# ReLU and row sums: the first 128 rows on 32 partitions, handled by VectorE alone

## The chip, the cores and the metric

The kernel runs on one core of a Trainium2 chip. The metric is the device time of one execution in microseconds (us), the median of several runs; less is better. The work is done by VectorE (DVE in the profile), ScalarE (ACT) and the DMA engines; SyncE (SP) only waits and issues transfers.

## The reference

```
x = np.random.randn(32, 512, 1024).astype(np.float32)

def reference(x):
    relu_x = np.maximum(x, 0)
    return np.sum(relu_x, axis=-1).astype(np.float32)
```

The input is 16,384 rows of 1,024 numbers, 67.1 MB. Each row is rectified and summed to one number; the output is 64 KB.

## The kernel before

Seen as 16,384 rows, the input is cut into three regions of 128 x 1, 128 x 111 and 128 x 16 rows (`REGIONS`). In each, partition p of the on-chip memory takes as many consecutive rows as the region has per partition: one, 111 or 16. The sums go to `res`, 128 partitions by 128 columns, and are stored from there.

**Loads.** Three big buffers (`buf[:, 0..2]`), each 16 rows per partition, are filled in turn by seven chunks (`CHUNKS`, line 94): chunk 0 is the first region's one row and 15 rows of the second region, in two DMAs; chunks 1 to 6 have 16 rows each. The remaining 16 rows per partition are the tail: pieces of 8, 4 and 2 rows (line 104), and two last rows cut into pieces of less than a row (lines 115 and 118), so that little is left to compute when the last bytes land. All loads are issued by SP on one queue. Chunks 0, 1 and 2 are issued at once; chunk 0's two DMAs are moved to the front of the program. From chunk 3 on, SP first waits until the reductions of the chunk that was in the same buffer are done (`s_dve`, line 90); the tail waits for chunk 4's.

**Compute.** In chunks 0 to 5, ScalarE rectifies several rows in place with one instruction (line 154, `ACT_STEPS`) and VectorE sums these rows with `tensor_reduce` (line 169, `DVE_STEPS`). In chunk 5 a few rows, and in chunk 6 and the tail all rows, are done one at a time, rectified and summed by one instruction, by either engine (`on_act`, line 130; `on_dve`, line 133).

**Stores.** The first region's sums lie in column 0 of `res`, one on each partition. VectorE transposes 32x32 blocks of `res` after chunk 1 (line 178), which puts the 128 sums into four rows of 32 in `turned`; SP waits for that (`s_turn`) behind the tail loads and stores four pieces of 128 B (line 120). It then waits for chunk 6 and the last load and stores the second region's columns (line 126), and at the very end the third region's (line 224). The program ends when all stores have landed.

Of the kernel before, what the change touches and what calls it, by code (L numbers as in the profile page):

```python
# [3 lines left out]
P = 128  # L4
D = 1024
BIG = 16
NB = 3
REGIONS = [1, 111, 16]
CHUNKS = [[(0, 0, 1), (1, 0, 15)]] + [[(1, 16 * c + 15, 16)] for c in range(6)]
ACT_STEPS = [[16], [7, 9], [7, 9], [7, 9], [4, 5, 7], [3, 4, 5]]  # L10
DVE_STEPS = [[16], [7, 4, 5], [7, 4, 5], [7, 4, 5], [4, 5, 7], [3, 4, 5]]
TAIL = [8, 4, 2]
CUT = 912
HEAD = 224
# [4 lines left out]
def bass_relu_sum_kernel(  # L19
# [14 lines left out]
    fp32 = mybir.dt.float32  # L34
    ALU = mybir.AluOpType
    AF = mybir.ActivationFunctionType
    X = mybir.AxisListType.X

    B, S, _ = x.shape
    J = B * S // P  # L40
    NBIG = len(CHUNKS)
    assert BIG * NBIG + sum(TAIL) + 2 == J == sum(REGIONS)

    xr = x.rearrange("b s d -> (b s) d")
    of = out.rearrange("b s -> (b s)")
    start = [sum(REGIONS[:i]) for i in range(len(REGIONS))]
    xv = [
        xr[P * s : P * (s + n), :].rearrange("(p j) d -> p j d", p=P)
        for s, n in zip(start, REGIONS)
    ]  # L50
    ov = [of[P * s : P * (s + n)].rearrange("(p j) -> p j", p=P) for s, n in zip(start, REGIONS)]

    buf = nc.alloc_sbuf_tensor("buf", [P, NB, BIG, D], fp32)
    w = D - CUT
    seam = nc.alloc_sbuf_tensor("seam", [P, 2 + w + HEAD + 3], fp32)
    res = nc.alloc_sbuf_tensor("res", [P, J], fp32)
    turned = nc.alloc_sbuf_tensor("turned", [P, 32], fp32)
    aside = nc.alloc_psum_tensor("aside", [P, 4 * D], fp32)

    n_in = NBIG + len(TAIL) + 3  # L60
    s_in = [nc.alloc_semaphore(f"s_in{i}") for i in range(n_in)]
    s_act = nc.alloc_semaphore("s_act")
    s_dve = nc.alloc_semaphore("s_dve")
# [2 lines left out]
    s_half = nc.alloc_semaphore("s_half")  # L66
    s_seam = nc.alloc_semaphore("s_seam")
    s_last = nc.alloc_semaphore("s_last")
    s_turn = nc.alloc_semaphore("s_turn")
    s_store = nc.alloc_semaphore("s_store")  # L70
    s_out = nc.alloc_semaphore("s_out")

    sp, act, dve = nc.sync, nc.scalar, nc.vector

    NTWO = len(ACT_STEPS)
    done = [sum(map(len, DVE_STEPS[: c + 1])) for c in range(NTWO)]

# [4 lines left out]
    code = nc.main_func.blocks[0].instructions  # L82
    arrival = next(
        i
        for i, ins in enumerate(code)
        if ins.engine == mybir.EngineType.SP and type(ins).__name__ == "InstDrain"
    )
    for c in range(NBIG + 1):
        if c >= NB:
            sp.wait_ge(s_dve, done[c - NB])  # L90
        if c < NBIG:
            i = 0
            for g, j, n in CHUNKS[c]:
                sp.dma_start(  # L94
                    out=buf[:, c % NB, i : i + n, :], in_=xv[g][:, j : j + n, :]
                ).then_inc(s_in[c], 16)
                i += n
                if c == 0:
                    code.insert(arrival, code.pop())
                    arrival += 1  # L100
    r = 0
    tail = []
    for i, n in enumerate(TAIL):
# [10 lines left out]
    for k, (lo, hi) in enumerate((first, second, third)):  # L114
# [1 line left out]
            s_in[NBIG + len(TAIL) + k], 16  # L116
        )
    sp.dma_start(out=seam[:, 2 : 2 + w + HEAD], in_=rows[:, CUT : D + HEAD]).then_inc(s_seam, 16)
    sp.wait_ge(s_turn, 1)
    sp.dma_start(  # L120
        out=of[0:P].rearrange("(k q) -> k q", q=32), in_=turned[0:P:32, 0:32]
    ).then_inc(s_store, 16)
    sp.wait_ge(s_fact, 1)
    sp.wait_ge(s_fdve, 1)
# [4 lines left out]
    def on_act(t, acc, to=None):  # L129
        return act.activation(t if to is None else to, t, AF.Relu, accum_out=acc)  # L130

    def on_dve(t, acc, to=None):
        return dve.tensor_scalar(  # L133
            out=t if to is None else to,
            in0=t,
            scalar1=0.0,
            scalar2=None,
            op0=ALU.max,
            op1=ALU.add,
            accum_out=acc,  # L140
        )

    def row(c, i):
        return buf[:, c % NB, i, :], res[:, c * BIG + i : c * BIG + i + 1]

    k = 0
    for c in range(NTWO):
        alone = BIG - sum(ACT_STEPS[c])
        act.wait_ge(s_in[c], 16 * len(CHUNKS[c]))
        r = 0  # L150
        ready = []
        for n in ACT_STEPS[c]:
            t = buf[:, c % NB, r : r + n, :]
            act.activation(t, t, AF.Relu).then_inc(s_act, 1)  # L154
            k += 1
            ready += [k] * n
            r += n
        for i in range(BIG - alone // 2, BIG):
            on_act(*row(c, i))
        if alone:  # L160
            dve.wait_ge(s_in[c], 16 * len(CHUNKS[c]))
            for i in range(BIG - alone, BIG - alone // 2):
                on_dve(*row(c, i))
        r = seen = 0
        for n in DVE_STEPS[c]:
            if ready[r + n - 1] > seen:
                seen = ready[r + n - 1]
                dve.wait_ge(s_act, seen)
            dve.tensor_reduce(  # L169
                out=res[:, c * BIG + r : c * BIG + r + n],  # L170
                in_=buf[:, c % NB, r : r + n, :],
                axis=X,
                op=ALU.add,
            ).then_inc(s_dve, 1)
            r += n
        if c == 1:
            dve.wait_ge(s_dve, done[c])
            dve.transpose(out=turned[:, :], in_=res[:, 0:32]).then_inc(s_turn, 1)  # L178


    j0 = NBIG * BIG
    for c in range(NTWO, NBIG):
        act.wait_ge(s_in[c], 16 * len(CHUNKS[c]))
        dve.wait_ge(s_in[c], 16 * len(CHUNKS[c]))
        for i in range(BIG):
            ins = (on_act if i % 2 else on_dve)(*row(c, i))
            if i >= BIG - 2:
                ins.then_inc(s_fact if i % 2 else s_fdve, 1)
# [16 lines left out]
    k = 2 + w  # L205
# [49 lines left out]
```

## Time and profile before

| | |
|---|---|
| median of 3 runs | 160.74 us (160.72 to 160.82) |
| the profiled execution | 160.78 us, of which the span shows 159.4 |
| VectorE busy | 120.7 us (76%) |
| ScalarE busy | 101.4 us (64%) |
| DMA queue of SP | 67.18 MB in 2,456 packets, 98.0% of the time of 16 DMA engines |
| first load (512 KB), issue to landing | 3.4 us |
| last load | lands at 156.84 us by the chain; VectorE's last addition starts at 157.53 |

The span runs from the first recorded instruction to the end of the last event; the run's time has 1.4 us more around it. A packet in the DMA records is one contiguous run of bytes that one of the 16 DMA engines moves: a load of n rows to each of 128 partitions has 128 packets of n x 4 KB. "SPq" is SP's issuing of a DMA; the time to landing counts from there and holds the wait in the queue behind earlier transfers.

### The profile page before, as it was taken

How to read it: one execution, taken by the hardware profiler on the slowest of the kernel's cores; microseconds unless marked ns; L12 is line 12 of the kernel's file. 1: busy time of each engine (PE TensorE's matmuls, PEld its weight loads, DVE VectorE, ACT ScalarE, POOL GpSimd, SP SyncE). 2: the span in 40 equal slices, each digit the busy share in tenths (PEclk: the TensorE clock that was granted, in tenths of full speed). 3: DMA queues.
4: the chain of work that ended last, by engine and by line, in shares of the span. 5: the costliest groups of instructions: out<-in, count | busy, mean ns of one | idle time of the engine just before them, and what ended most of it. 6: DMA issues, size and time to landing. Idle time of an engine off the chain costs nothing.

```text
span 159.4 us, 150 instructions
## 1 busy us (share of the span) xinstructions
DVE 120.7 (76%) x59; ACT 101.4 (64%) x54; POOL 0.2 (0%) x4
## 2 busy tenths in 40 slices
DVE  0000000009999999999999999999999999898995
ACT  3000059990799808996099951999329990496975
POOL 0000000000000000000000000000000000000000
DMA  9997996996997998989969969969969979798994
GB/s 378 493 401 339 493 526 263 526 526 263 526 460 329 526 411 378 526 362 428 526 296 493 526 263 526 526 263 526 510 280 526 444 345 526 304 485 366 423 399 146
DMA packets 2457, 67.18 MB, mean 421 GB/s; under 512 B 536, under 2 KB 792, under 8 KB 1176
## 3 DMA queue, kind: packets, MB, share of 16 engines
q1 hardware_dynamic: 2456, 67.18, 98.0%
q14 instruction: 1, 0.01, 0.0%
HBM read 67.11 MB, written 0.07 MB: 421 GB/s over the span
## 4 chain that ended last, share of the span: by engine, by line
DVE 54%; DMA 34%; ACT 9%; SPq 1%; issue 0%
DVE res L169 54%; DMA buf<-in_x_dram 34%; ACT buf L154 9%; SPq L104 1%; SPq L115 0%; DVE seam L133 0%; SPq L94 0%; ACT aside L130 0%; DVE turned L178 0%
## 5 line engine op out<-in xcount | busy, mean ns | idle before, releaser
L169 DVE TENSOR_REDUCE res<-buf 128x4 f32<-128x4096 f32 (+4 forms) x16 | 99.3, 6276 | 35.6 <-ACT buf L154 35.6
L154 ACT ACTIVATE buf<-buf 128x7168 f32<-128x7168 f32 (+5 forms) x13 | 80.4, 6233 | 46.2 <-DMA buf<-in_x_dram 46.2
L133 DVE TENSOR_SCALAR_CACHE_REDUCE buf<-buf 128x1024 f32<-128x1024 f32 (+3 forms) x20 | 20.9, 1100 | 1.6 <-DMA buf<-in_x_dram 1.4
L130 ACT ACTIVATE buf<-buf 128x1024 f32<-128x1024 f32 x14 | 14.6, 1042 | 7.9 <-DMA buf<-in_x_dram 7.9
L130 ACT ACTIVATE aside<-buf 128x1024 f32<-128x1024 f32 (+2 forms) x5 | 4.1, 828 | 1.1 <-DMA buf<-in_x_dram 1.0
L130 ACT ACTIVATION_READ_ACCUMULATOR buf<-buf 128x1 f32 x14 | 2.6, 186 | 0.0
L154 ACT ACT_TABLE_LOAD x1 | 1.3, 1283 | 1.3 <-PEq L240 1.3
L133 DVE DVE_READ_ACCUMULATOR buf<-buf 128x1 f32 x20 | 1.7, 83 | 0.0
L130 ACT ACTIVATION_READ_ACCUMULATOR aside<-buf 128x1 f32 x5 | 0.9, 187 | 0.0
L133 DVE TENSOR_SCALAR_CACHE_REDUCE seam<-seam 128x227 f32<-128x227 f32 x1 | 0.4, 391 | 0.0
L130 ACT ACTIVATE aside<-seam 128x114 f32<-128x114 f32 x1 | 0.3, 270 | 0.0
L178 DVE STREAM_TRANSPOSE turned<-res 128x32 f32<-128x32 f32 x1 | 0.2, 213 | 0.0
L130 ACT ACTIVATION_READ_ACCUMULATOR aside<-seam 128x1 f32 x1 | 0.2, 186 | 0.0
L240 POOL MEMSET const-bfloat16-1.0<- 128x1 bf16 x1 | 0.1, 102 | 0.0
L240 POOL MEMSET const-uint8-127<- 128x1 uint8 x1 | 0.1, 102 | 0.0
L240 POOL MEMSET const-float32-1.0<- 128x1 f32 x1 | 0.1, 99 | 0.0
L240 POOL MEMSET const-float32-0.0<- 128x1 f32 x1 | 0.1, 98 | 0.2 <-issue 0.2
L133 DVE DVE_READ_ACCUMULATOR seam<-seam 128x1 f32 x1 | 0.1, 82 | 0.0
## 6 DMA issues: line engine op xcount, KB each, us to landing
buf<-in_x_dram SPq DMA_DIRECT2D x1, 7680.0 KB, 21.2
buf<-in_x_dram SPq DMA_DIRECT2D x1, 4096.0 KB, 25.5
buf<-in_x_dram SPq DMA_DIRECT2D x1, 2048.0 KB, 30.0
buf<-in_x_dram SPq DMA_DIRECT2D x1, 1024.0 KB, 32.0
buf<-in_x_dram SPq DMA_DIRECT2D x1, 512.0 KB, 3.4
buf<-in_x_dram SPq DMA_DIRECT2D x1, 456.0 KB, 32.6
buf<-in_x_dram SPq DMA_DIRECT2D x1, 312.0 KB, 33.0
seam<-in_x_dram SPq DMA_DIRECT2D x1, 168.0 KB, 32.6
```

The source lines that it names most:

```text
L104: sp.dma_start(out=buf[:, tb, r : r + n, :], in_=xv[-1][:, r : r + n, :]).then_inc(s_in[NBIG + i], 16)
L130: return act.activation(t if to is None else to, t, AF.Relu, accum_out=acc)
L133: return dve.tensor_scalar(out=t if to is None else to, in0=t, scalar1=0.0, scalar2=None, op0=ALU.max, op1=ALU.add, accum_out=acc,)
L154: act.activation(t, t, AF.Relu).then_inc(s_act, 1)
L169: dve.tensor_reduce(out=res[:, c * BIG + r : c * BIG + r + n], in_=buf[:, c % NB, r : r + n, :], axis=X, op=ALU.add,).then_inc(s_dve, 1)
L178: dve.transpose(out=turned[:, :], in_=res[:, 0:32]).then_inc(s_turn, 1)
L240: nc = _bacc.Bacc("TRN2", target_bir_lowering=False, num_devices=1)
```

## The change

The first 128 rows are no longer a part of chunk 0, one row to each of 128 partitions. They are loaded first of all into partitions 0 to 31, four consecutive rows (16 KB) to each, in the first part of buffer 2, which chunk 2 fills later. VectorE alone handles them, with two instructions: a `tensor_scalar` that rectifies all four rows of the 32 partitions in place, and a `tensor_reduce` that sums them into `lead`, 32 partitions by four numbers. Neither ScalarE nor a transpose is needed for them, and SP stores `lead` in 32 pieces of 16 B at the place where it stored `turned`. Chunk 0 keeps its 15 rows of the second region in one DMA, so ScalarE and VectorE handle 15 rows there instead of 16. SP now waits, before it issues chunk 2's load, until VectorE has done the two instructions (`s_led`). The loads at the front of the program are this lead load and chunk 0's.

```diff
-CHUNKS = [[(0, 0, 1), (1, 0, 15)]] + [[(1, 16 * c + 15, 16)] for c in range(6)]
-ACT_STEPS = [[16], [7, 9], ...
-DVE_STEPS = [[16], [7, 4, 5], ...
+LEAD = 4
+CHUNKS = [(1, 0, 15)] + [(1, 16 * c + 15, 16) for c in range(6)]
+ACT_STEPS = [[15], [7, 9], ...
+DVE_STEPS = [[15], [7, 4, 5], ...
...
+    leaders = P // LEAD
+    fore = buf[:leaders, NB - 1, :LEAD, :]
+    sp.dma_start(
+        out=fore, in_=xr[:P, :].rearrange("(p j) d -> p j d", j=LEAD)
+    ).then_inc(s_lead, 16)
+    ahead()
     for c in range(NBIG + 1):
+        if c == NB - 1:
+            sp.wait_ge(s_led, 2)
         if c >= NB:
             sp.wait_ge(s_dve, done[c - NB])
         if c < NBIG:
-            i = 0
-            for g, j, n in CHUNKS[c]:
-                sp.dma_start(
-                    out=buf[:, c % NB, i : i + n, :], in_=xv[g][:, j : j + n, :]
-                ).then_inc(s_in[c], 16)
-                i += n
-                if c == 0:
-                    code.insert(arrival, code.pop())
-                    arrival += 1
+            g, j, n = CHUNKS[c]
+            sp.dma_start(
+                out=buf[:, c % NB, BIG - n :, :], in_=xv[g][:, j : j + n, :]
+            ).then_inc(s_in[c], 16)
+            if c == 0:
+                ahead()
...
-    sp.wait_ge(s_turn, 1)
     sp.dma_start(
-        out=of[0:P].rearrange("(k q) -> k q", q=32), in_=turned[0:P:32, 0:32]
+        out=of[:P].rearrange("(p j) -> p j", j=LEAD), in_=lead[:leaders, :]
     ).then_inc(s_store, 16)
...
+    dve.wait_ge(s_lead, 16)
+    dve.tensor_scalar(out=fore, in0=fore, scalar1=0.0, scalar2=None, op0=ALU.max).then_inc(s_led, 1)
+    dve.wait_ge(s_led, 1)
+    dve.tensor_reduce(out=lead[:leaders, :], in_=fore, axis=X, op=ALU.add).then_inc(s_led, 1)
+
     k = 0
     for c in range(NTWO):
...
-        if c == 1:
-            dve.wait_ge(s_dve, done[c])
-            dve.transpose(out=turned[:, :], in_=res[:, 0:32]).then_inc(s_turn, 1)
```

`ahead()` does what the two removed lines did: it moves the DMA just written to the front of the program. The new local names `bare` and `ready = [0] * bare` only shift chunk 0's rows by one place in its buffer.

More of the change, by code (lines that the diff above doesn't have):

```diff
@@ L8 @@
 REGIONS = [1, 111, 16]
-CHUNKS = [[(0, 0, 1), (1, 0, 15)]] + [[(1, 16 * c + 15, 16)] for c in range(6)]
-ACT_STEPS = [[16], [7, 9], [7, 9], [7, 9], [4, 5, 7], [3, 4, 5]]
-DVE_STEPS = [[16], [7, 4, 5], [7, 4, 5], [7, 4, 5], [4, 5, 7], [3, 4, 5]]
+LEAD = 4
+CHUNKS = [(1, 0, 15)] + [(1, 16 * c + 15, 16) for c in range(6)]
+ACT_STEPS = [[15], [7, 9], [7, 9], [7, 9], [4, 5, 7], [3, 4, 5]]
+DVE_STEPS = [[15], [7, 4, 5], [7, 4, 5], [7, 4, 5], [4, 5, 7], [3, 4, 5]]
 TAIL = [8, 4, 2]
@@ L56, in bass_relu_sum_kernel @@
     res = nc.alloc_sbuf_tensor("res", [P, J], fp32)
-    turned = nc.alloc_sbuf_tensor("turned", [P, 32], fp32)
+    lead = nc.alloc_sbuf_tensor("lead", [P, LEAD], fp32)
     aside = nc.alloc_psum_tensor("aside", [P, 4 * D], fp32)
@@ L68, in bass_relu_sum_kernel @@
     s_last = nc.alloc_semaphore("s_last")
-    s_turn = nc.alloc_semaphore("s_turn")
+    s_lead = nc.alloc_semaphore("s_lead")
+    s_led = nc.alloc_semaphore("s_led")
     s_store = nc.alloc_semaphore("s_store")
@@ L87, in bass_relu_sum_kernel, with ahead @@
     )
+    def ahead():
+        nonlocal arrival
+        code.insert(arrival, code.pop())
+        arrival += 1
+    leaders = P // LEAD
[4 more added lines that the diff above has]
+    ahead()
     for c in range(NBIG + 1):
+        if c == NB - 1:
+            sp.wait_ge(s_led, 2)
         if c >= NB:
@@ L144, in row @@
         return buf[:, c % NB, i, :], res[:, c * BIG + i : c * BIG + i + 1]
+    dve.wait_ge(s_lead, 16)
+    dve.tensor_scalar(out=fore, in0=fore, scalar1=0.0, scalar2=None, op0=ALU.max).then_inc(s_led, 1)
+    dve.wait_ge(s_led, 1)
+    dve.tensor_reduce(out=lead[:leaders, :], in_=fore, axis=X, op=ALU.add).then_inc(s_led, 1)
     k = 0
     for c in range(NTWO):
[L148 to L151, printed above, removed]
+        bare = BIG - CHUNKS[c][2]
+        alone = BIG - bare - sum(ACT_STEPS[c])
+        act.wait_ge(s_in[c], 16)
+        r = bare
+        ready = [0] * bare
         for n in ACT_STEPS[c]:
@@ L160, in bass_relu_sum_kernel @@
         if alone:
-            dve.wait_ge(s_in[c], 16 * len(CHUNKS[c]))
+            dve.wait_ge(s_in[c], 16)
             for i in range(BIG - alone, BIG - alone // 2):
                 on_dve(*row(c, i))
-        r = seen = 0
+        r, seen = bare, 0
         for n in DVE_STEPS[c]:
@@ L175, in bass_relu_sum_kernel @@
             r += n
-        if c == 1:
-            dve.wait_ge(s_dve, done[c])
-            dve.transpose(out=turned[:, :], in_=res[:, 0:32]).then_inc(s_turn, 1)
     j0 = NBIG * BIG
     for c in range(NTWO, NBIG):
-        act.wait_ge(s_in[c], 16 * len(CHUNKS[c]))
-        dve.wait_ge(s_in[c], 16 * len(CHUNKS[c]))
+        act.wait_ge(s_in[c], 16)
+        dve.wait_ge(s_in[c], 16)
         for i in range(BIG):
```

## The prediction

> **What bounds the kernel now.** I read the page's slices and DMA queue first, then the chain that ended last, then the stretches, and last the packet records of the trace. From the page, with DMA the mean busy share of the 16 DMA engines in tenths and GB/s what they moved, slice by slice:
>
> ```profile
> span 159.4 us, 150 instructions
> DVE 120.7 (76%) x59; ACT 101.4 (64%) x54; POOL 0.2 (0%) x4
> DMA  9997996996997998989969969969969979798994
> q1 hardware_dynamic: 2456, 67.18, 98.0%
> ```
>
> VectorE and ScalarE have room, and the queue's packets take 98.0% of 16 engines' time. The sixes and sevens in the slices are no pauses: a packet can be longer than half a slice (65,536 B take 2.42 us, a slice is 4 us), and it is booked where it starts. The stretches, which are longer than a packet, show it plainly (columns: length, VectorE, ScalarE, GpSimd, clock, DMA share, GB/s):
>
> ```profile
> 3.00:22.00 19.00, 0.00 (x0) 0.30 (x1) 0.00 (x0) 1.00 0.97 421
> 42.00:61.00 19.00, 19.00 (x3) 13.59 (x3) 0.00 (x0) 1.00 1.02 442
> 100.00:119.00 19.00, 19.00 (x4) 13.70 (x4) 0.00 (x0) 1.00 1.02 442
> 138.00:157.00 19.00, 17.95 (x33) 16.62 (x33) 0.00 (x0) 1.00 0.98 414
> ```
>
> The DMA share is 0.97 to 1.02 from the third microsecond to the last landing, whatever the two engines do. The chain that ended last (start, length, what) seems to say something else:
>
> ```profile
> 0.43 21.24 DMA buf<-in_x_dram
> 21.70 13.87 ACT buf L154
> 35.59 34.48 DVE res L169 x4
> ...
> 122.04 0.33 SPq L104
> ...
> 123.86 32.98 DMA buf<-in_x_dram
> ...
> 157.53 0.40 DVE seam L133 x2
> ```
>
> It goes through VectorE for 86 us because the SP queue holds the tail loads until VectorE frees their buffer at 122.0. But the last of those loads takes 33 us to land: it stands behind chunk 6, whose last 64 KB packet ends at 137.40 in the packet records, and behind the rest of the tail. The tail is issued 15 us before the queue could begin it. So VectorE is no bound; the bytes are. In the packet records the 16 engines' streams run without gaps from their first chunk-0 packet (starts 2.61 to 3.07) to that end: matched into streams, each has 56 packets of chunks 0 to 6 and takes 134.3 to 134.8 us for them. What an engine loses at the start it keeps to the end.
>
> **The first load.** Before, 128 rows go to 128 partitions: 128 packets of 4,096 B, eight to an engine, median 159 ns, so 8 x 0.159 = 1.272 us an engine. After, the same 512 KB are 32 packets of 16,384 B. The same size occurs in the tail's 2 MB load (four rows to each of 128 partitions): 0.611 us each. What matters is how many engines, or ways into the 32 partitions, can work at full rate at once. The trace has no load to fewer than 128 partitions, so I bound it by even deals of the 32 packets:
> - all 16 ways: 2 x 0.611 = 1.222 us, 0.05 less than before;
> - eight ways: 4 x 0.611 = 2.444 us, 1.17 more;
> - four ways, which is what 32 partitions get if an engine always has eight of them: 8 x 0.611 = 4.888 us, 3.62 more.
>
> I take eight ways. The ends are far apart; the row that it is nearest to is the packet row itself: every packet from 16 KB up moves at 26.8 to 27.1 GB/s, so one way has one fixed speed, and a quarter of the partitions can hardly offer all sixteen ways, while four ways would need the deal of a 128-row load to be kept for a list of 32. The middle deal is one halving from each end. All streams behind the first load move by this amount, since none has a gap to take it up. Only the stagger of the starts (0.46 us between the first and the last engine) could swallow some, if the engines that are held are the early ones: then 0.7 instead of 1.17.
>
> [...]
>
> **VectorE's new head.** It waits for the first load, rectifies 32x4096 in place and sums it. The nearest row for the first is the 128x1024 max-and-add at 1,216 ns: four of these are 4.9 us, and without a sum kept it may be less. The reduction is the row 128x4096, 4.41 us. VectorE had nothing to do until 35.59, so both are covered. What is queued behind that wait on VectorE is chunk 0's reduction, not due before 35 us. The load lands at 3.4 us now, so at some 4.6 then, and the head ends by about 14.
>
> **The new wait before chunk 2.** SP now holds chunk 2's load until the head is done (it used to be issued within the first 2.1 us), and all SP issues behind it queue with it. Ahead of it in the DMA queue are 15.5 MB of chunks 0 and 1, which last until about 41.7. Issued at 14, it has 27 us of cover: nothing. Without that cover each microsecond of delay would be one on the end.
>
> **Chunk 0 has 15 rows.** ScalarE's 128x16384 takes 13.86 us and VectorE's reduction of it 17.22; a row less saves about 0.85 (at the rate of the rows 128x7168 in 6.17 and 128x9216 in 7.87) and 1.06 (128x4096 in 4.41 against 128x7168 in 7.60). The landing comes 1.17 later, so buffer 0 is free 0.7 us earlier, at about 52.1, and what follows on VectorE is earlier by that and by the transpose (0.21). The loads that it releases are issued 7 to 15 us before the queue reaches them. What is late next is the DMA queue, which is late already: no gain.
>
> **The store.** SP's wait for the transpose goes; it had passed at 70 us. The store is issued behind the tail loads as before. Instead of four packets of 128 B (13 ns each) it has 32 of 16 B; the nearest records, 64 B, take 11 ns: two on each engine, 0.02 us, behind the last load, whose last packet ends at 157.03. The next store's packets begin at 158.01. Nothing on the end; if all 32 went one after the other on one engine, 0.35 us would still fit in that gap. Its landing is waited for only with the last store's, whose packets are 2 us behind.
>
> **The sum.** The span's 159.4 + 1.17 = 160.6; around it lie 160.78 - 159.4 = 1.4, so 161.95 for that execution. It stands 0.04 above the median of 160.74, which gives 161.9.
>
> **Rivals.**
> - *Even deal at full rate.* All 16 engines write their two packets at 27 GB/s. For it: before, each engine gets an equal part of every load. Against: it needs 32 partitions to take in as much as 128. Time: 160.74 - 0.05 = 160.7, no change that can be told.
> - *A shorter run-up, faster.* The first packets start at 1.02 and the streams reach chunk 0 at 2.61 to 3.07; eight packets of 159 ns alone would bring them there at 2.29. So 0.32 to 0.78 us go on run-up (the first four packets take over 0.70 us each). If 32 large packets are laid out sooner than 128 small ones and are taken in at full rate, most of it comes back: about -0.55, 160.2. It decides only if the even deal holds too and over 0.32 us of run-up goes. Against: a first answer from memory is waited for in both.
> - *Four ways.* 160.74 + 3.62 = 164.4. For it: eight packets to an engine is the deal of all full loads. Against: nothing requires that deal for 32 partitions.
> - *The held chunk 2* is no rival of weight: it costs from the point at which VectorE's head ends after 41 us, three times what its rows add up to.
>
> **How the numbers follow.** Eight ways 0.80, even deal 0.09, shorter run-up 0.06, four ways 0.05. The likeliest gives 161.9. Its low end takes in the stagger and a load that overlaps partly with chunk 0 (down to 161.1), its high end packets with stalls (chunk 0 has some of 2.45 to 2.52 us where 2.27 is usual), so 162.3. That leaves out the other three cases, 0.20 together, and is the range. Faster or slower counts from 0.2%, 0.32 us, about what a measurement of this kernel can tell from no change: faster 0.06, same 0.09, slower 0.85.
>
> **What would show it.** In the packet records: 32 packets of 16,384 B at the start that take about 1.2 us each where the tail's take 0.61, or run at 0.61 on eight engines only; chunk 0's packets starting around 3.8 to 4.2 on the late engines; all chunk landings, seen by ScalarE's first instructions at 21.7, 41.05, 60.4, 79.8, 99.1 and 118.45, later by 1.2; no new gap at chunk 2; 2.6 us from the last landing to the end, as before. Landings where they were, with 0.61 us packets, would mean the even deal; landings earlier by 0.3 or more, the run-up. A gap in the streams near 41 us would mean that the wait before chunk 2 was mispriced, and a longer end after the last landing that the 16 B stores were.

## The result and the profile after

The changed kernel takes 161.62 us (median of 6 runs, 161.49 to 161.79) against 160.74 before: 0.88 us more, a ratio of 1.0055 with a 95% interval of 1.0042 to 1.0068. The forecast was 161.9, with a range of 161.1 to 162.3. The profiled execution took 161.72, 0.94 more than the one before.

The page after; the same four rows as before (span, VectorE, DMA share by slices, SP's DMA queue):

```profile
span 160.4 us, 151 instructions
DVE 126.3 (79%) x60; ACT 100.6 (63%) x54; POOL 0.2 (0%) x4
DMA  9599969969969969969969969969989899698994
q1 hardware_dynamic: 2400, 67.18, 98.1%
```

VectorE has 5.6 us more work, ScalarE 0.8 less, and the DMA queue is as full as it was. The stretches (length, VectorE, ScalarE, GpSimd, clock, DMA share, GB/s) have the same rates as before, too:

```profile
42.00:61.00 19.00, 19.00 (x3) 13.75 (x2) 0.00 (x0) 1.00 1.02 442
100.00:119.00 19.00, 19.00 (x4) 13.89 (x3) 0.00 (x0) 1.00 1.02 442
138.00:157.00 19.00, 17.56 (x31) 16.23 (x31) 0.00 (x0) 1.00 0.98 415
```

So nothing runs slower in the middle. The head of the kernel, in the timeline (start, length, engine, line):

```profile
0.42 11.05 SPq L108 DMA_DIRECT2D buf<-in_x_dram  x3
...
4.40 2.28 DVE L158 TENSOR_SCALAR buf<-buf 32x4096 f32<-32x4096 f32 x1 [4.40 <-DMA buf<-in_x_dram]
6.71 4.41 DVE L160 TENSOR_REDUCE lead<-buf 32x4 f32<-32x4096 f32 x1
```

VectorE begins at 4.40, a microsecond after the first load used to land (3.4 us from its issue; now 4.4), and is done at 11.1. SP issues chunk 2 then (the end of the row of 11.05 us). The chain that ended last:

```profile
0.42 22.01 DMA buf<-in_x_dram
22.46 13.01 ACT buf L171
35.49 16.16 DVE res L186
...
123.37 34.23 DMA buf<-in_x_dram
...
158.29 0.40 DVE seam L144 x2
```

Chunk 0 lands 0.76 us later than before (22.46 against 21.70 for ScalarE's start), and VectorE's last addition starts 0.76 later (158.29 against 157.53). The delay is there at the first big landing and stays as it is. From that last addition to the span's end it was 1.89 us before and is 2.07 now: there is a second, small loss at the very end. It stands in SP's waits (engine, line, what it waited for; total, times, longest), here the last one, for the stores to land, before:

```profile
SPq L226 <- DMA out_dram<-res: 1.1, 1, 1.1
```

and after:

```profile
SPq L108 <- DVE lead L160: 9.6, 1, 9.6
SPq L240 <- DMA out_dram<-res: 1.3, 1, 1.3
```

The first of these two is the new wait before chunk 2; it holds SP for 9.6 us and no transfer: in the packet records no stream has a gap near 41 us, where chunk 2 begins.

**The packet records.** After, 32 packets of 16,384 B are at the start, two on each of 16 streams, all 16 at once. They take 0.80 to 1.25 us each; the same size takes 0.61 in the tail. The first packet of chunk 0 behind them takes 2.65 to 2.89 us instead of about 2.27, on every stream: a part of the delay shows only there. I measure the start by one number, the *run-in*: from the first packet's start to the mean end of the 16 first chunk-0 packets, less the 2.268 us that such a packet usually takes. Before it is 1.83 us, after 2.71: 0.88 more (0.87 by the clock of the span). The last of these 16 packets ends at 5.335 before and 6.071 after, 0.74 later; the last packet of the last load at 157.027 and 157.772, 0.745 later. From there to the span's end it is 2.392 and 2.586, 0.194 longer. 0.745 + 0.194 = 0.94, the difference of the two profiled executions. In the repetition told below the run-in is 2.79, and the last packet ends 0.83 later than before.

### The profile page after: what moved, and what is told of

Same layout as the page of the kernel before. It is cut to its first block, busy times and chain, and to the rows that moved or that the text cites. A ratio compares the mean times of both kernels' runs of the same rounds, so it can differ in the third digit from the quotient of the medians.

```text
span 160.4 us, 151 instructions
## 1 busy us (share of the span) xinstructions
DVE 126.3 (79%) x60; ACT 100.6 (63%) x54; POOL 0.2 (0%) x4
## 4 chain that ended last, share of the span: by engine, by line
DMA 53%; DVE 27%; ACT 17%; SPq 1%; issue 1%
DMA buf<-in_x_dram 53%; DVE res L186 27%; ACT buf L171 17%; SPq L116 1%; SPq L127 0%; DVE seam L144 0%; SPq L97 0%; ACT aside L141 0%
## 5 line engine op out<-in xcount | busy, mean ns | idle before, releaser
L171 ACT ACTIVATE buf<-buf 128x7168 f32<-128x7168 f32 (+5 forms) x13 | 79.5, 6167 | 47.8 <-DMA buf<-in_x_dram 47.8
L158 DVE TENSOR_SCALAR buf<-buf 32x4096 f32<-32x4096 f32 x1 | 2.3, 2281 | 4.4 <-DMA buf<-in_x_dram 4.4
L160 DVE TENSOR_REDUCE lead<-buf 32x4 f32<-32x4096 f32 x1 | 4.4, 4407 | 0.0
```

Of the source, the lines that this page charges most:

```text
L158: dve.tensor_scalar(out=fore, in0=fore, scalar1=0.0, scalar2=None, op0=ALU.max).then_inc(s_led, 1)
L160: dve.tensor_reduce(out=lead[:leaders, :], in_=fore, axis=X, op=ALU.add).then_inc(s_led, 1)
```

## The experiments

All were timed beside the kernel before, which had medians of 160.80 to 160.86 in these runs. Times are medians of four to six executions, but for the last experiment; run-ins, packets and ends are those of the one profiled execution of each. The "end" is the time from the last load packet's end to the span's end.

**Is it the ways into the memory, or the number of partitions?** Two runs with the same 64 packets of 8 KB, on two choices of 64 partitions, and one on 16 partitions:

```diff
-LEAD = 4
+LEAD = 2        # partitions 0 to 63;   LEAD = 8: partitions 0 to 15
...
-    fore = buf[:leaders, NB - 1, :LEAD, :]
+    fore = buf[32:96, NB - 1, :LEAD, :]     # the other 64: two halves for VectorE, four instructions
```

Partitions 0 to 63: 

> The lead rows go to partitions 0 to 63, two rows (8 KB) each, everything else as in the change. Theory A (the partitions that are written reach only some of the ways into the memory, and 0 to 63 reach the same eight as 0 to 31): no better than the change, 161.6 us (161.4 to 161.8), 8 KB packets of about 0.6 us instead of 0.31. Theory B (the loss comes from too few partitions or too large packets): half of the change's 0.88 us is won back, 161.2.

Partitions 32 to 95: 

> The lead rows go to partitions 32 to 95, two rows (8 KB) each; VectorE does them in two halves of 32 partitions (four instructions instead of two). Same number of partitions and packets as in the run on 0 to 63. Theory A: the two halves reach all sixteen ways, so 8 KB packets take about 0.31 us as in the tail, and the loss goes: 160.5 to 160.8 us. Theory B: the same as on 0 to 63, 161.2.

Partitions 0 to 15: 

> The lead rows go to partitions 0 to 15, eight rows (32 KB) each: 16 packets, one for each engine. Theory A: four ways, 4.8 us for 512 KB where eight take 2.4, so 2.4 us above the change: 164.0 us. Theory B (loss by the number of partitions, half as many, but all engines still at work): between 161.6 and 162.5.

Measured: 163.98, 162.99 and 163.68 us. By their totals the first two fit neither theory, so their expectations of the time failed; the third is 2.1 above the change, where theory A had 2.4. Two other things came with 64 partitions. Their first packet starts at 1.39 and 1.41 us where all others start between 1.01 and 1.11 (SP's issue takes 0.57 and 0.63 us, not 0.38; why, I can't say), and their ends are 4.96 and 3.85 us long (below). On 32 to 95 an instruction load during the tail comes on top (below). The run-in is free of all three:

| first load | packets | run-in, us | packets alone by the ways, us (an estimate from the median times of one packet before: 0.159, 0.309, 0.611 and 1.213 for 4, 8, 16 and 32 KB) |
|---|---|---|---|
| 128 partitions (the kernel before; four runs told below) | 128 x 4 KB | 1.83; 1.82, 1.82, 1.73, 1.84 | 16 ways: 8 x 0.159 = 1.27 |
| 32 to 95 | 64 x 8 KB | 1.77 | 16 ways: 4 x 0.309 = 1.24 |
| 0 to 63 | 64 x 8 KB | 2.62 | 8 ways: 8 x 0.309 = 2.47 |
| 0 to 31 (after) | 32 x 16 KB | 2.71 | 8 ways: 4 x 0.611 = 2.44 |
| 0 to 31 (the narrow load told below) | 128 x 4 KB | 2.77 | 8 ways: 16 x 0.159 = 2.54 |
| 0 to 15 | 16 x 32 KB | 4.89 | 4 ways: 4 x 1.213 = 4.85 |

Partitions 0 to 63 are as slow as 0 to 31, and 32 to 95 as quick as all 128, with the same number and size of packets: their median is 0.309 us on 32 to 95, the tail's own time, and 0.44 on 0 to 63 (0.6 was expected; the rest shows on chunk 0's first packets behind them, 2.60 to 2.94 us instead of 2.27). And 128 packets of 4 KB, as in the kernel before, are as slow on 0 to 31 as 32 packets of 16 KB. So neither the number of partitions nor the number and size of the packets makes the loss: theory B is out, for the loads, and what fits all rows is theory A: the run-in goes by which partitions are written, as if 0 to 31 and 0 to 63 had eight ways, 0 to 15 four and 32 to 95 all sixteen. The records name no ways; that there are such, and how many, is an estimate from the run-ins and packet times of these rows. It is not a matter of idle engines: 16 of the 32 packets start within 0.34 us, ahead of any other, so all 16 streams are at work on the narrow load from the start.

**Does the store cost the second loss?**

```diff
-    sp.dma_start(
-        out=of[:P].rearrange("(p j) -> p j", j=LEAD), in_=lead[:leaders, :]
-    ).then_inc(s_store, 16)
```

> The change without its store of the 128 lead sums: these 128 outputs are left unwritten. After the change the loads end 0.75 us later and the span 0.94. If the 32 pieces of 16 B make the last stores land later: 0.2 less than the change, 161.4 us, and 1.4 us for the last store's landing. If not: as the change, 161.6, and 1.6 us.

Measured: 161.60 us, a ratio of 1.0050 (1.0036 to 1.0064), so the expected time of 161.4 was missed; but the end is 2.43 us, and SP's last wait is back at

```profile
SPq L237 <- DMA out_dram<-res: 1.1, 1, 1.1
```

The median is 0.79 above that of the kernel before, where the change has 0.88, and 1.10 in its repetition. The end says that the store costs 0.2; the medians are too near to each other to confirm it by themselves, and the loads of this run end 0.07 later than the change's.

**What are small pieces worth, and can the store go elsewhere?** One run stores the lead sums early, one undoes the spread and the store, one stores 128 pieces of 4 B, and the change was run again beside them:

```diff
 # the early store: ahead of chunk 2, not behind the tail
+            sp.dma_start(
+                out=of[:P].rearrange("(p j) -> p j", j=LEAD), in_=lead[:leaders, :]
+            ).then_inc(s_store, 16)
 # both runs on 128 partitions: one row to each, sums into res[:, 0:1]
-LEAD = 4
+LEAD = 1
 # the one: transposed after chunk 1 and stored from turned[0:P:32, 0:32], as before
 # the other:
-        out=of[:P].rearrange("(p j) -> p j", j=LEAD), in_=lead[:leaders, :]
+        out=of[:P].rearrange("(p j) -> p j", j=LEAD), in_=res[:, 0:1]
```

Early store: 

> The change, with the store of the lead sums issued before chunk 2 (SP waits for these sums there anyway) and not behind the tail. Theory C (the small pieces occupy the write side and hold back the landing of the last stores by what is left of them at the end): from the last load packet's end to the span's end 2.4 us as without the store, not 2.59; 161.4 to 161.5 us. If the pieces hold back the loads behind them in the queue instead: 161.6 or more. The loads' delay at the start stays: last load packet at 157.7 to 157.8.

128 partitions, transposed: 

> The change with only the spread of the lead rows and their store undone: one row to each of 128 partitions, VectorE alone rectifies and sums them, SP waits for that before chunk 2, the sums are transposed and stored in four pieces of 128 B as before. Ways theory: nothing of the loss is left, 160.7 to 160.9 us, chunk 0's load lands at about 21.7. If VectorE's head or the new wait cost anything, more than 160.9.

128 partitions, untransposed: 

> As the run on 128 partitions, but the 128 sums are stored untransposed, as 128 pieces of 4 B, at the old place behind the tail. Theory C with a price for each piece (64 pieces of 8 B made the time from the last load to the end 3.85 and 4.96 us long, 32 pieces of 16 B 2.59, 16 pieces of 32 B 2.44): from 5 to 10 us from the last load to the end, 163.5 to 168 us. If what counts is not the number of pieces but something of the 64 partitions, 160.8.

The change again: 

> The change itself once more, on the chip of these runs, as the base for them: 161.6 us, 0.8 to 0.9 above the kernel before.

The change again: 161.96 us (1.0051 to 1.0077; 161.6 was expected), its end 2.76 us, the last wait 1.4. The untransposed store: 166.36 us (ratio 1.0347, 1.0320 to 1.0374), its end 7.81, and

```profile
SPq L240 <- DMA out_dram<-res: 6.5, 1, 6.5
```

With the 64 pieces of the first run the same line reads

```profile
SPq L240 <- DMA out_dram<-res: 3.7, 1, 3.7
```

The ends, all for the same 512 B of sums: no store 2.43, four pieces 2.39, 16 pieces 2.44, 32 pieces 2.59 and 2.76, 64 pieces 3.85 and 4.96, 128 pieces 7.81. The packets themselves take 9 ns each from 32 B down, and 13 ns for 128 B. The last store has 128 pieces of 64 B and lands in 1.4 us when nothing small is ahead of it, so it isn't the count alone: what costs here is many pieces of 16 B or less. Count and size change together in these runs, so they don't tell the two apart.

When the pieces go out matters too. In the last experiment below the same 32 pieces begin 0.83 us before the last load's end, not 0.22 (the change) or 0.14 (its repetition), and there, in its one execution, the end is 2.41 and SP's last wait 1.1: they cost nothing. From the first piece's packet to the span's end it is 2.81 and 2.90 us with 32 pieces, and 5.28 and 4.97 with 64. So something after the packets takes longer with more pieces, and delays the end only by what is left of it then. What it is, no run shows.

The early store takes the 0.2 off the end (2.41 us) but the time is 162.13 us, no better than the change beside it (161.96), so the expectation of 161.4 to 161.5 failed and its alternative came true. Its last load packet ends at 158.36, not at 157.7 to 157.8, and 0.51 later than that of the repetition. Of this 0.15 is there before the pieces, in the run-in (2.94 against 2.79). Its 16 B pieces lie at 41.12 to 41.65 us, and 13 of the 16 load packets that start next, at 43.5 to 44.2, take up to 0.61 us longer than their usual 2.42, 4.25 us together, 0.27 for each of 16 streams; in the change and its repetition no packet at this place does. So in this run the small pieces held the loads behind them, too.

**The run on 128 partitions**, transposed, was expected at 160.7 to 160.9 and took 161.47 us, so the expectation failed. Its loads are level with the kernel before up to the last packet of chunk 6 (137.297 against 137.398). Then, at 151.54, its DMA records have an instruction load of 8,192 B, which takes 0.31 us, and the 8 KB packet of the tail that starts as it ends takes 0.92 us instead of 0.31. Its last load packet ends 0.54 us later than before. In the kernel before such a load comes at 159.31, after everything. The run on 32 to 95 has one at 151.97, with the same effect. These two have the longest programs for VectorE, waits counted: 73 and 74 instructions, against 69 before and 71 in the change. Two runs put this to the test:

```diff
 # the run on 128 partitions, VectorE's program shortened to 70
-DVE_STEPS = [[15], [7, 4, 5], [7, 4, 5], [7, 4, 5], [4, 5, 7], [3, 4, 5]]
+DVE_STEPS = [[15], [7, 9], [7, 9], [7, 9], [4, 5, 7], [3, 4, 5]]
 # the kernel before, VectorE's program lengthened to 73
-DVE_STEPS = [[16], [7, 4, 5], [7, 4, 5], [7, 4, 5], [4, 5, 7], [3, 4, 5]]
+DVE_STEPS = [[16], [7, 4, 3, 2], [7, 4, 3, 2], [7, 4, 3, 2], [4, 5, 4, 3], [3, 4, 5]]
```

> The run on 128 partitions lost 0.6 us although its loads were level with the kernel before up to chunk 6; in its DMA records an instruction load of 8,192 B starts at 151.54, and one 8 KB packet of the tail takes 0.92 us instead of 0.31 just then. In the kernel before and in the change that instruction load comes after the last load. VectorE's program has 73 instructions there, waits counted, 69 before and 71 in the change. Here three of VectorE's reductions are merged with the next (chunks 1 to 3: 7 and 9 rows, not 7, 4 and 5), which makes 70. Theory D (the longer program makes VectorE fetch code while the tail is loaded): the instruction load moves behind the last load and the time is 160.75 to 160.95 us. If VectorE's head or the wait before chunk 2 costs it: 161.4 as before this edit.

> The kernel before with four of VectorE's reductions cut in two (chunks 1 to 4), so that its program has 73 instructions instead of 69; nothing else. Theory D: an instruction load of 8,192 B at about 151 to 152 us, one DMA engine held by 0.6 us, 161.3 to 161.5 us. If the length of the program does not matter: 160.8 us, for VectorE has the time for four more instructions.

The lengthened kernel before: 161.68 us (1.0038 to 1.0064), 0.88 more, a little above what was expected. Its instruction load is at 151.15, the 16 KB packet behind it takes 1.25 us instead of 0.61, and its last load packet ends 0.77 later. Four more instructions on an engine that has time for them cost as much as the whole change. The chain's end in it:

```profile
123.99 33.60 DMA buf<-in_x_dram
...
158.28 0.40 DVE seam L133 x2
```

The shortened run on 128 partitions, against that:

```profile
122.64 34.21 DMA buf<-in_x_dram
...
157.55 0.40 DVE seam L146 x2
```

Its last addition starts at 157.55, where the kernel before has 157.53, and its spans are 159.4 to 159.6 like those of the kernel before (159.3 to 159.6 in nine of its ten executions). The instruction load is no longer among the loads, as expected. So VectorE's lead work (on 128 partitions here), the wait before chunk 2 and the 15-row chunk cost nothing inside the span. Its time is 161.37 us all the same, and the expected 160.75 to 160.95 failed: 1.90 us lie outside the span (median; 1.5 to 2.0), where it is 1.38 in the kernel before. Two instruction loads are recorded there, at 161.00 and 161.09, and the next run, which also has 1.88 us outside, has two as well. In both SP's program has one instruction more than before (39 for 38); the run with 73 instructions on VectorE has that too, but 1.38 outside. Whose loads these are, and whether they cost the half microsecond, stays open.

**The narrow load with the old store.**

```diff
-        out=fore, in_=xr[:P, :].rearrange("(p j) d -> p j d", j=LEAD)
+        out=fore, in_=xr[:P, :].rearrange("(j p) d -> p j d", j=LEAD)
...
+    dve.transpose(out=turned[:, :], in_=lead[:, :]).then_inc(s_turn, 1)
...
-        out=of[:P].rearrange("(p j) -> p j", j=LEAD), in_=lead[:leaders, :]
+        out=of[:P].rearrange("(j p) -> j p", j=LEAD), in_=turned[:LEAD, :]
```

> The change's load on 32 partitions with the store of the kernel before: partition p takes rows p, 32+p, 64+p and 96+p (4 KB packets, about 0.3 us each), the sums are transposed and stored in four pieces of 128 B; VectorE's reductions in chunks 1 to 4 are merged so that its program stays short. Ways theory and theory C together: the loads end 0.75 to 0.85 us later than before, the end after the last load is 2.4 us and not 2.6 to 2.75: 161.5 to 161.65 us, 0.1 to 0.35 under the change on the same chip.

Measured: 162.63 us, so the expectation failed, through my own edit. The merged reductions, meant to keep the program short, made VectorE late; it and not the loads ends the chain:

```profile
127.62 12.98 DVE res L194 x3
140.60 18.20 DVE buf L148 x36
```

and 0.5 us more than before are outside the span, as said. What it does show: the last wait for the stores is 1.1 us again with four pieces of 128 B, and the run-in is 2.77, within the 2.71 to 2.94 of the other loads to partitions 0 to 31, though its packets are those of the kernel before, 128 of 4 KB. It does not settle the sum.

**The cover of the new wait.**

```diff
-            sp.wait_ge(s_led, 2)
+            sp.wait_ge(s_dve, 1)
```

> The change with chunk 2's load held longer: SP waits for chunk 0's reduction (done at 51.6) and not for the lead sums (done at 11.1). The DMA queue should run dry when chunk 1's last packet ends at about 41.2 and start again 0.6 to 1 us after the issue, at some 52.5: a gap of 11 to 11.5 us that the end shows in full, 172.6 to 173.3 us. If the loads could make up for a gap, less.

Measured: 174.37 us in a single execution, 1.1 above the expected 172.6 to 173.3. The stretches (same columns as above):

```profile
43.00:52.00 9.00, 9.00 (x2) 9.00 (x2) 0.00 (x0) 1.00 0.00 0
56.00:72.00 16.00, 13.09 (x3) 0.00 (x0) 0.00 (x0) 1.00 1.02 442
```

The queue is dry from 41.5, moves nothing through the whole first stretch, and starts again at 52.8, 0.95 us after the issue at 51.88. The gap is 11.6 us on average over the streams (41.35 to 52.97), the first packets behind it take about 0.7 longer, and the last loads end 12.5 later than in the repetition of the change (mean 170.35 against 157.81). The time shows all of it, 12.4 us on 161.96, and with it a run-up that I had not put in, which is why the expectation was too low.

## Why the prediction was right, and where its steps were off

**The DMA queue bounds the kernel.** Held. The delay of the first landing is the delay of the last, 0.76 us in the chain both times, and a gap made on purpose came back in full.

**The first load, eight ways.** The loss came, and the runs on 0 to 63 and 32 to 95 (run-ins of 2.62 and 1.77 us) tie it to the partitions, apart from number and size of the packets. That it would be eight ways was an estimate: nothing in the trace before told eight from sixteen or four. The size was off: 1.17 was predicted, 0.88 in the run-in and 0.745 on the last packet were measured (0.83 in the repetition). The term that was mis-sized is the run-up, which the sum left unchanged. Before, 0.56 us of the run-in are not packets (1.83 - 1.27); with eight ways 0.27 (2.71 - 2.44), with four 0.04. So 0.29 us of the 1.17 were in the run-in before already. Where the run-up went, no run shows; the rows of the table say only that less of it is left over, the fewer the ways. The other 0.13 is the stagger, which the text had named: the mean of the 16 streams ends 0.84 later, the last one 0.745, for the streams that were first are held longest, and the first chunk-0 packets end within 0.21 us of each other instead of 0.41. The packets were expected at 1.2 us each and took 0.80 to 1.25, with the rest booked on chunk 0's first packets.

**The store: nothing.** Wrong, by 0.19 us in the profiled execution and 0.37 in that of the repetition; only in the run without the cover, where the pieces went out earlier, was it nothing. The step that failed took the packet's own time (11 ns for 64 B) as the price of a piece; what it costs shows in SP's last wait, for the landing (1.3 us, 1.4 in the repetition, against 1.1), and in no packet. The longer end is the sign that the prediction had named for this. The other way out that was named, that the landing is waited for with the last store's alone, is where the cost came in: it holds that one up. The two mis-sizings were of opposite sign: 0.43 too much for the load, 0.19 too little for the store. That they partly cancel is luck; it is why the total came within 0.3 us of 161.9.

**VectorE's head, the wait, 15 rows.** Held: the head ends at 11.1 (about 14 was predicted; its first instruction took 2.28 us, where four rows of the max-and-add had given 4.9), ScalarE's instruction takes 13.00 and VectorE's 16.15 us, buffer 0 is free at 51.66 (52.1 predicted), and inside the span none of it costs anything (the run with the shortened program). That the wait would cost at least a microsecond for each microsecond without its cover is shown by the run that took it away. The 15.5 MB ahead of chunk 2 are 16.3 in the units of the profile, which changes nothing, since the 41.7 us come from the landings.

**The rivals.** The even deal and the shorter run-up are out for partitions 0 to 31 by packets of 0.80 to 1.25 us, where the tail's take 0.61, and by a run-in that grew. Four ways came true on 16 partitions (4.89 us, where four ways alone give 4.85).

No version here beats the kernel before. The nearest, on 128 partitions with the short program, is level with it inside the span.

## What to carry to other kernels

In a kernel bound by its loads, as this one, a slow first transfer is paid by every byte behind it: chunk 0 landed 0.76 us later, and the last addition started 0.76 later. It was slow here on partitions 0 to 31 and 0 to 63, which lost 0.8 to 1.1 us of run-in, and on 0 to 15, which lost 3.1; 32 to 95 lost none. So spread even a small first load over all 128 partitions; fewer and larger packets didn't make up for it (2.71 us of run-in with 32 of 16 KB on 0 to 31, 2.77 with 128 of 4 KB). Store sums in few larger pieces, even at the price of a transpose: for the same 512 B, four pieces of 128 B and 16 of 32 B cost nothing on the end, 128 of 4 B cost 5.4 us, and the transpose takes 0.2 us of VectorE. When an edit that touches no bottleneck moves the time by half a microsecond, look in the DMA records for instruction loads before explaining it.

## What the hardware did that I had not expected

An instruction load of 8 KB held up the data. In three runs one took 0.31 us while the tail was loaded, the one load packet that started as it ended took 0.61 to 0.64 us longer than usual, and the last load ended 0.54 and 0.77 us later in the two of them that can be compared. The length of VectorE's program decided it: at 69 to 71 instructions there was none during the loads, at 73 and 74 there was one, at 151 to 152 us; adding four brought it, taking three away removed it. With 16 engines that have no gap, these loads were not hidden.

The store of 32 pieces held SP for 5.84 us at its issue in the change (5.78 in the repetition, 5.87 without the cover; 0.64 for the four pieces before, 1.05 for 64). Nobody waits for SP at that point, and I have no reason for it.
